# Weight-block sums moved from VectorE and ScalarE to GpSimd in a hybrid decoder step

## The chip, the cores and the metric

The kernel runs on one core of a Trainium2 chip. A core has five engines with an instruction queue each: TensorE (PE in the profile) multiplies matrices from SBUF into PSUM, VectorE (DVE) and ScalarE (ACT) work on tiles element by element, GpSimd (POOL) also works on tiles and issues DMA transfers, SyncE (SP) issues DMA transfers. The engines run side by side and wait for each other through semaphores; each takes its own queue in order.

The metric is the device time of one execution in microseconds, as the median of several runs. The profile is that of one execution.

## The reference

One inference step of one decoder layer, for a prompt of 2048 rows and for 8 sample rows with given states; the model width is 1024:

```python
hn = _rmsnorm(x, g_norm) * (1.0 + scale[:, None]) + shift[:, None]
z = hn @ w_in                      # columns: xa, za (RG-LRU), q, k, v, glr, zg (gated linear attention)
...
y_lru = h.astype(x.dtype) * jax.nn.silu(za)
...
y_gla = o.reshape(Bn, T, D_GLA).astype(x.dtype) * jax.nn.silu(zg)
mix = jnp.concatenate([y_lru, y_gla], axis=-1) @ w_out
x = x + gate[:, None] * mix
```

All is float32 with a close tolerance. `w_in` is 1024 x 5136, `w_out` is 2048 x 1024. Between the two products stand a short convolution, two gates and a recurrence (group one), and a chunked causal attention with decay (group two).

## The kernel before

**Precision.** A float32 product is made of three fast products: each operand is split into a high part (a cast to a rounded type, `F32R`) and a low part (the operand less its high part), and high x high, high x low and low x high are added up in PSUM. So a "split" of a tile is a cast and a subtraction.

**Fewer products.** Some matrix products are done on 2 x 2 blocks with seven block products in place of eight. That needs sums and differences of weight blocks, split like everything else. They are prepared on the side, early in the program, and written to DRAM, from where later stages load them:

- `pair_weights` (line 764) prepares five pairs of input-weight column tiles. For each pair it loads the four blocks b11, b21, b12, b22 (each 128 x 512) into the tile `tr`, forms four differences in place (line 776), and splits each of the four results: cast into `th` (line 781), subtraction in place (line 782), and two DMAs to the DRAM tile `twd` (line 784). The blocks are read again from about 610 us on.
- `out_weights` (line 800) prepares the output weights in 16 steps s = 0 to 15. A step loads two row tiles of `w_out` into `r` (line 829), multiplies them by the gate `g` (two operations on 512 columns, line 850), forms four differences on 256 columns (line 850, into `t` and `r`), and writes seven blocks to the DRAM tile `wd` (line 864). Every step with s // 4 odd (eight of them) also splits two blocks: casts into `p` (line 854), subtractions (line 855), DMAs to `wd2` (line 857). Before steps 0, 7 and 8 the gate is loaded again and its bias added (line 815).

**The order of the work.** The program is written out by Python and the order on each engine follows mostly from the order of writing, with a planner that may move what is ready. Side work is put in by a clock of the writing, not of the chip: every projection (24 products of 128 x 512 or less) advances it by one unit or half a unit (`tick`), and `after(units, f)` calls `f` at the first tick at or past the time asked for. `pair_weights` and `out_weights` are chains of such calls: load, four units later the first group of operations, then the next. Step s + 1 loads when step s has issued its stores; the tiles `r` and `t` have one buffer.

Two helpers tie side work to a place in another engine's queue. Both take the last instruction written so far for that engine as the mark:

```python
def behind(q):
    return tc.issue_after(next(x for x in reversed(list(nc.cur_bb.bb.instructions)) if x.engine == q.engine))
...
def held(q):
    mark = next(x for x in reversed(list(traced)) if x.engine == q.engine)
    ...
    for x in list(traced):
        if id(x) not in before and x.engine in (SP.engine, G.engine):
            tc.add_manual_dep(x, mark.name, ...DependencyClass.Sync...)
```

`behind(V)` keeps a VectorE instruction from being planned ahead of the VectorE instruction written before it; it adds no wait. `held(V)` makes each SyncE and GpSimd instruction of its block wait by semaphore for that VectorE instruction.

**The stages in time.** First half of the rows: four heads of attention, each followed by some tiles of the recurrence. The pairs are prepared from 77 us on (loads at 77.3 to 279.9 us), the steps follow from 310.9 us. Before the second half the memory is laid out anew (`open_sp`, line 1460): the tiles of steps and pairs end, and the first block of the second half, `fs`, lies where `r` and `p` were. `next_hn` (line 1428) fills it through `modulate` (lines 197 to 205): transposes on PE, scaling on ACT (lines 199 and 201) or DVE (203), a cast on GpSimd (204), the low part on DVE (205). Then come the seven-product stages of the second half (line 1567, products at 1561), which read `twd`; then the second half's attention heads with the remaining steps; then the output product (line 1846), which reads `wd` and `wd2`.

**What else the lines in this text are.** Lines 147 to 153 are a reciprocal square root in some eleven tiny DVE operations, 181 scales rows by it, 228 and 225 are the low part and the cast of the first half. The attention's chain is 999 (running sum of the decay), 1027 (scaled queries), 1042 (products of queries and keys), 1049 (low part of the masked scores), 1072 to 1077 (output and state products and the state's update), 1081 (output copied from PSUM), 1089 (its norm), 1162 (its transposes). The samples' chain runs over 1098 and 1100 (loads issued by GpSimd), 1105, 1114, 1124 to the product in line 1164. The gate columns come back through line 1210, a GpSimd DMA. Line 1303 is the low part of the convolution's output.

Of the kernel before, what the change touches and what calls it, by code (L numbers as in the profile page):

```python
# [8 lines left out]
F32 = mybir.dt.float32  # L9
# [3 lines left out]
OP = mybir.AluOpType  # L13
# [36 lines left out]
def dram(ap, off, pattern):  # L50
    return bass.AP(tensor=ap.tensor, offset=ap.offset + off, ap=pattern)
# [3 lines left out]
def hybrid_kernel(ctx, tc, i, o):  # L55
    nc = tc.nc
    V, S, G, PE, SP = nc.vector, nc.scalar, nc.gpsimd, nc.tensor, nc.sync
# [623 lines left out]
    def behind(q):  # L681

        return tc.issue_after(next(x for x in reversed(list(nc.cur_bb.bb.instructions)) if x.engine == q.engine))


    @contextmanager
    def held(q):

        traced = nc.cur_bb.bb.instructions
        mark = next(x for x in reversed(list(traced)) if x.engine == q.engine)  # L690
        before = {id(x) for x in traced}
        yield
        for x in list(traced):
            if id(x) not in before and x.engine in (SP.engine, G.engine):
                tc.add_manual_dep(x, mark.name, mybir.DependencyInfo(
                    mybir.DependencyClass.Sync, mybir.DependencyReason.DATA), reason="held")
# [4 lines left out]
    def after(units, fn, gla=False, val=False):  # L701
        clock[1] += 1
        heapq.heappush(pend, (clock[0] + units, clock[1], fn, gla, val))
# [46 lines left out]
    def ready(what):  # L750
        nonlocal hp
        waiting.remove(what)
        if what == "pairs":
            hpx.close()
            hp = hpx.enter_context(tc.tile_pool(name="hp", bufs=1, reuse_waits="tile"))
        if not waiting:
            out_weights()

    def zpairs():

        return ([(ZG + 2 * h * P, ZG + (2 * h + 1) * P) for h in HEADS[1:]]
                + [(ZA + j * P, XA + j * P) for j in EARLY])

    def pair_weights(n=0):

        cols = zpairs()
        if n == len(cols):
            ready("pairs")
            return
        r = hp.tile([P, 2, KT, P], F32, tag="tr", name="tr")  # L770
        for a, col in enumerate(cols[n]):
            G.dma_start(r[:, a], i["w_in"][0, :, col:col + P].rearrange("(k p) n -> p k n", p=P))
        b11, b21, b12, b22 = r[:, 0, :4], r[:, 0, 4:], r[:, 1, :4], r[:, 1, 4:]

        def sub(x, y, z):
            return lambda: V.tensor_tensor(x, y, z, op=OP.subtract)

        def split(k, x):
            def f():
                t = hp.tile([P, 4, P], F32R, tag="th", name="th", bufs=2)  # L780
                S.copy(t, x)
                V.tensor_tensor(x, x, t.bitcast(F32), op=OP.subtract)
                for u, y in enumerate((t.bitcast(F32), x)):
                    G.dma_start(twd[n, k, :, u], y.rearrange("p k n -> p (k n)"))
            return f

        def one(ops):
            for f in ops[0]:
                with behind(V):
                    f()  # L790
            if ops[1:]:
                after(0.5, lambda: one(ops[1:]))
            else:
                pair_weights(n + 1)

        halves = [split(k, x) for k, x in enumerate((b11, b22, b12, b21))]
        after(4, lambda: one([[sub(b11, b12, b11), sub(b12, b22, b12), sub(b22, b22, b11), sub(b21, b21, b22)],
                                halves[:2], halves[2:]]))

    def out_weights(s0=0):  # L800


        def begin(s):
            q = s // 8
            outw["busy"] = True

            g = hp.tile([P, 2, 256], F32, tag="g", name="g")
            bt = hp.tile([P, 2, 256], F32, tag="t", name="bt")
            G.dma_start(g, dram(gated, (8 + 32 * q) * 256, [[0, P], [64 * 256, 2], [1, 256]]))
            G.dma_start(bt, dram(i["b_ada"], 2 * D + q * 256, [[0, P], [512, 2], [1, 256]]))  # L810
            r = load(s)

            def add():
                with behind(V):
                    V.tensor_tensor(g, g, bt, op=OP.add)
                after(0.5, lambda: step(s, r, g))

            after(4, add)

        def where(s):  # L820

            return s // 8, s // 4 % 2, s % 4

        def load(s):
            q, f, m = where(s)
            r = hp.tile([P, 2, 2, 256], F32, tag="r", name="r")
            for a in range(2):
                k = CTS[f] + 4 * a + m
                G.dma_start(r[:, a], i["w_out"][0, k * P:(k + 1) * P].rearrange("p (b n) -> p b n", b=2)[:, :, q * 256:q * 256 + 256])
            return r  # L830

        def one(ops, end):


            with behind(V):
                for f in ops[0]:
                    f()
            if ops[1:]:
                after(0.5, lambda: one(ops[1:], end))
            else:  # L840
                end()

        def step(s, r, g):
            t = hp.tile([P, 3, 256], F32, tag="t", name="t")
            b11, b12, b21, b22 = r[:, 0, 0], r[:, 0, 1], r[:, 1, 0], r[:, 1, 1]
            q, f, m = where(s)
            c = slice(q * 256, q * 256 + 256)

            def op(*a):
                return lambda: V.tensor_tensor(*a[:3], op=a[3])  # L850

            def split(n, x):
                p = hp.tile([P, 2, 256], F32R, tag="p", name="p", bufs=2)
                S.copy(p[:, 0], x)
                V.tensor_tensor(p[:, 1], x, p[:, 0].bitcast(F32), op=OP.subtract)
                for h in range(2):
                    G.dma_start(wd2[n, :, h, m, c], p[:, h].bitcast(F32))

            def store():

                for x, ops in ((r[:, 0], (B11, T1)), (r[:, 1], (B21, B22)), (t, (T2, T3, T4))):
                    for n, k in enumerate(ops):
                        if not (f and k in (B22, T4)):
                            G.dma_start(wd[f, k, :, m, c], x[:, n])
                if outw["stop"] or s == 15:
                    outw["busy"], outw["next"] = False, s + 1
                elif s % 8 < 7:
                    again(s + 1, g)
                elif q == 0:
                    begin(s + 1)  # L870

            one([[op(r[:, 0], r[:, 0], g, OP.mult), op(r[:, 1], r[:, 1], g, OP.mult)],
                 [op(t[:, 1], b22, b12, OP.subtract), op(b12, b12, b11, OP.subtract),
                  op(t[:, 0], b22, b12, OP.subtract), op(t[:, 2], b21, t[:, 0], OP.subtract)]]
                + ([[lambda: split(0, b22), lambda: split(1, t[:, 2])]] if f else []), store)

        def again(s, g):
            r = load(s)
            after(4, lambda: step(s, r, g))

        begin(s0)
# [846 lines left out]
    class Pair:  # L1728
# [157 lines left out]
        def end(self, t):  # L1886
            V.scalar_tensor_tensor(self.z[t], self.z[t], self.r[:, t:t + 1], gfin, op0=OP.mult, op1=OP.mult)
# [288 lines left out]
    for n in range(2, 16):  # L2176
        g = n - 1
        x, prev = pairs[n], pairs[n - 1]
# [16 lines left out]
    for q in range(8):  # L2195
        g, k = 2 + q // 2, q % 2
# [63 lines left out]
```

## Time and profile before

| | us |
|---|---|
| median of 3 runs | 1455.29 (1455.26 to 1460.6) |
| the profiled execution's own time | 1454.69 |
| its span, first to last instruction | 1452.9 |

| engine | busy us | share of the span |
|---|---|---|
| PE | 1424.1 | 98% |
| PE weight load | 1250.8 | 86% |
| DVE | 1051.5 | 72% |
| ACT | 689.6 | 47% |
| POOL | 220.0 | 15% |

The granted clock of TensorE is 0.998 over the run. Busy time of POOL counts both its arithmetic and the making of its DMA issues (about 0.54 us each for the stores of lines 784, 857 and 864). A row of a group gives its line, engine, operation, the tiles written and read, the shape and the count; a row of a line's own view gives the durations as min/median/max in ns and the first and last start in us. A row of waits names who waited, for whom, and then the total in us, the count and the longest. A wait is put down to the instruction that ended it last.

### The profile page before, as it was taken

How to read it: one execution, taken by the hardware profiler on the slowest of the kernel's cores; microseconds unless marked ns; L12 is line 12 of the kernel's file. 1: busy time of each engine (PE TensorE's matmuls, PEld its weight loads, DVE VectorE, ACT ScalarE, POOL GpSimd, SP SyncE). 2: the span in 40 equal slices, each digit the busy share in tenths (PEclk: the TensorE clock that was granted, in tenths of full speed). 3: DMA queues.
4: the chain of work that ended last, by engine and by line, in shares of the span. 5: the costliest groups of instructions: out<-in, count | busy, mean ns of one | idle time of the engine just before them, and what ended most of it. 6: DMA issues, size and time to landing. Idle time of an engine off the chain costs nothing. (4 is left out here: it accounts for less than half of the span.)

```text
span 1452.9 us, 23584 instructions
## 1 busy us (share of the span) xinstructions
PE 1424.1 (98%) x8741; PEld 1250.8 (86%) x8741; DVE 1051.5 (72%) x2477; ACT 689.6 (47%) x1251; POOL 220.0 (15%) x364
## 2 busy tenths in 40 slices
PE   7999999999999999999999999999999999999998
PEld 5888989899898988778999999999998887788886
DVE  5757657776676688955468687586788986688886
ACT  4644544662545358524353454535557622144342
POOL 0200111212122113100212322323100000000000
PEclk9999999999999999999999999999999999999999
DMA  9755775764666455667846565656562767694453
GB/s 328 268 185 175 260 262 203 249 236 165 199 209 203 148 179 207 207 221 237 292 158 201 186 217 184 220 186 209 184 226 83 276 221 272 232 362 131 139 171 116
DMA packets 161752, 305.33 MB, mean 210 GB/s; under 512 B 12962, under 2 KB 91458, under 8 KB 159197
## 3 DMA queue, kind: packets, MB, share of 16 engines
q1 hardware_dynamic: 106837, 217.39, 43.6%
q0 software_dynamic: 22752, 70.44, 14.3%
q10 hardware_dynamic: 32048, 16.00, 3.7%
q8 instruction: 69, 1.13, 0.3%
q14 instruction: 46, 0.38, 0.1%
HBM read 188.51 MB, written 115.33 MB: 209 GB/s over the span
## 5 line engine op out<-in xcount | busy, mean ns | idle before, releaser
L661 PE MATMUL acc<-hh,w 128*128 128x512 f32 (+3 forms) x1112 | 386.1, 347 | 0.5 <-DVE xb L999 0.2
L662 PE MATMUL acc<-hl,w 128*128 128x512 f32 (+3 forms) x1112 | 375.6, 338 | 0.2 <-DVE hl L205 0.2
L663 PE MATMUL acc<-hh,w 128*128 128x512 f32 (+3 forms) x1112 | 375.1, 337 | 0.0
L662 PEld LDWEIGHTS acc<-hl,w 128*128 128x128 f32 x1112 | 209.3, 188 | 18.1 <-issue 1.2
L661 PEld LDWEIGHTS acc<-hh,w 128*128 128x128 f32 x1112 | 209.2, 188 | 18.1 <-ACT tx L1318 0.9
L663 PEld LDWEIGHTS acc<-hh,w 128*128 128x128 f32 x1112 | 209.1, 188 | 16.3
L1846 PE MATMUL acc<-w,a 128*128 128x512 f32 (+1 forms) x792 | 184.8, 386 | 0.0
L1846 PEld LDWEIGHTS acc<-w,a 128*128 128x128 f32 x792 | 146.8, 188 | 33.2 <-issue 3.4
L346 PE MATMUL acc<-w,hh 128*128 128x256 f32 (+1 forms) x508 | 144.7, 285 | 0.0
L348 PE MATMUL acc<-w,hl 128*128 128x256 f32 (+1 forms) x508 | 143.5, 282 | 0.2 <-DVE hl L228 0.2
L347 PE MATMUL acc<-w,hh 128*128 128x256 f32 (+1 forms) x508 | 143.4, 282 | 0.0
L1846 PE MATMUL tp<-w,a 128*128 128x512 f32 x564 | 136.0, 391 | 0.0
L1846 PEld LDWEIGHTS tp<-w,a 128*128 128x128 f32 x564 | 105.2, 188 | 26.8 <-issue 5.2
L346 PEld LDWEIGHTS acc<-w,hh 128*128 128x128 f32 x508 | 95.5, 188 | 1.3 <-ACT zs L1128 0.4
L348 PEld LDWEIGHTS acc<-w,hl 128*128 128x128 f32 x508 | 96.2, 189 | 0.4 <-DVE hl L228 0.4
L347 PEld LDWEIGHTS acc<-w,hh 128*128 128x128 f32 x508 | 96.0, 189 | 0.2
L1128 ACT ACTIVATE zs<-acc 128x512 f32<-128x512 f32 (+3 forms) x70 | 34.3, 490 | 107.0 <-PE acc L663 104.0
L1696 ACT CAST a<-s 128x512 fp32r<-128x512 f32 x61 | 36.5, 619 | 96.1 <-issue 36.6
L1278 DVE SCALAR_TENSOR_TENSOR cv<-xa,vecT,cv 128x512 f32<-128x512 f32 (+2 forms) x120 | 76.3, 638 | 7.2 <-ACT cv L1276 6.7
L1129 DVE SCALAR_TENSOR_TENSOR zs<-zs,acc 128x512 f32<-128x512 f32 (+3 forms) x70 | 38.4, 548 | 46.7 <-ACT zs L1128 46.7
L957 ACT CAST vh<-acc 128x256 fp32r<-128x256 f32 x56 | 20.5, 369 | 94.2 <-PE acc L348 81.8
L958 DVE TENSOR_TENSOR vl<-acc,vh 128x256 fp32r<-128x256 f32 x56 | 23.3, 420 | 51.1 <-ACT vh L957 51.1
(403 smaller groups left out, 2746.4 us busy)
## 6 DMA issues: line engine op xcount, KB each, us to landing
parts<-w SPq DMA_DIRECT2D x37, 1024.0 KB
w<-parts SPq DMA_DIRECT2D x28, 1024.0 KB
wr<-in_w_in_dram SPq DMA_DIRECT2D x38, 512.0 KB
a<-mixd SPq DMA_DIRECT2D x63, 256.0 KB
w<-wd SPq DMA_DIRECT2D x12, 1024.0 KB
w<-twd SPq DMA_DIRECT2D x20, 512.0 KB
mixd<-zs ACTq DMA_DIRECT2D x34, 256.0 KB
wada<-in_w_ada_dram SPq DMA_DIRECT2D x16, 512.0 KB
```

The source lines that it names most:

```text
L346: PE.matmul(ps, hh[:, kt, c], hi[:, kt % 4], start=kt == 0, stop=False)
L347: PE.matmul(ps, hh[:, kt, c], lo[:, kt % 4], start=False, stop=False)
L348: PE.matmul(ps, hl[:, kt, c], hi[:, kt % 4], start=False, stop=kt == KT - 1)
L661: PE.matmul(ps[:, :n], hi[:, kt], a, start=kt == 0, stop=False)
L662: PE.matmul(ps[:, :n], hi[:, kt], b, start=False, stop=False)
L663: PE.matmul(ps[:, :n], lo[:, kt], a, start=False, stop=kt == KT - 1)
L958: V.tensor_tensor(lo, ps[:, :DV], hi.bitcast(F32), op=OP.subtract)
L1128: S.activation(z, ps, AF.Tanh, scale=0.5)
L1129: V.scalar_tensor_tensor(z, z, 1.0, ps, op0=OP.add, op1=OP.mult)
L1278: V.scalar_tensor_tensor(cv[:, cq], xa[:, cq.start + k:cq.stop + k], cw[k], cv[:, cq], op0=OP.mult, op1=OP.add)
L1696: S.copy(t[:, 0, k], (low(t) if src is None else src)[:, k])
L1846: PE.matmul(ps, t[:, u, k], w[:, v, k, c], start=(q < 3 or ps is own) and (k, u, v) == (0, 0, 0), stop=(k, u) == (3, 1), skip_group_check= ...
```

## The change

The four differences and the four splits of a pair, and all arithmetic of an output-weight step, are issued to GpSimd. A cast, which was a copy by ScalarE, becomes a GpSimd `tensor_scalar` that multiplies by 1.0 and adds 0.0. The blocks are written under `held(V)` instead of `behind(V)`: each GpSimd instruction in them, the DMA issues included, waits for the VectorE instruction written last before the block. In the pairs a whole group stands in one such block, and the groups follow each other after one unit of the clock instead of half a unit. Tiles, shapes, loads and stores stay as they are.

```diff
--- before.py
+++ after.py
@@ -773,23 +773,23 @@
         b11, b21, b12, b22 = r[:, 0, :4], r[:, 0, 4:], r[:, 1, :4], r[:, 1, 4:]
 
         def sub(x, y, z):
-            return lambda: V.tensor_tensor(x, y, z, op=OP.subtract)
+            return lambda: G.tensor_tensor(x, y, z, op=OP.subtract)
 
         def split(k, x):
             def f():
                 t = hp.tile([P, 4, P], F32R, tag="th", name="th", bufs=2)
-                S.copy(t, x)
-                V.tensor_tensor(x, x, t.bitcast(F32), op=OP.subtract)
+                G.tensor_scalar(t, x, 1.0, 0.0, op0=OP.mult, op1=OP.add)
+                G.tensor_tensor(x, x, t.bitcast(F32), op=OP.subtract)
                 for u, y in enumerate((t.bitcast(F32), x)):
                     G.dma_start(twd[n, k, :, u], y.rearrange("p k n -> p (k n)"))
             return f
 
         def one(ops):
-            for f in ops[0]:
-                with behind(V):
+            with held(V):
+                for f in ops[0]:
                     f()
             if ops[1:]:
-                after(0.5, lambda: one(ops[1:]))
+                after(1, lambda: one(ops[1:]))
             else:
                 pair_weights(n + 1)
 
@@ -811,8 +811,8 @@
             r = load(s)
 
             def add():
-                with behind(V):
-                    V.tensor_tensor(g, g, bt, op=OP.add)
+                with held(V):
+                    G.tensor_tensor(g, g, bt, op=OP.add)
                 after(0.5, lambda: step(s, r, g))
 
             after(4, add)
@@ -832,7 +832,7 @@
         def one(ops, end):
 
 
-            with behind(V):
+            with held(V):
                 for f in ops[0]:
                     f()
             if ops[1:]:
@@ -847,12 +847,12 @@
             c = slice(q * 256, q * 256 + 256)
 
             def op(*a):
-                return lambda: V.tensor_tensor(*a[:3], op=a[3])
+                return lambda: G.tensor_tensor(*a[:3], op=a[3])
 
             def split(n, x):
                 p = hp.tile([P, 2, 256], F32R, tag="p", name="p", bufs=2)
-                S.copy(p[:, 0], x)
-                V.tensor_tensor(p[:, 1], x, p[:, 0].bitcast(F32), op=OP.subtract)
+                G.tensor_scalar(p[:, 0], x, 1.0, 0.0, op0=OP.mult, op1=OP.add)
+                G.tensor_tensor(p[:, 1], x, p[:, 0].bitcast(F32), op=OP.subtract)
                 for h in range(2):
                     G.dma_start(wd2[n, :, h, m, c], p[:, h].bitcast(F32))
```

## The prediction

> **What bounds the kernel now.** I read the page first (part 1), then the busy time of each engine by stage, then the list of who made TensorE wait, then the rows of the lines that move.
>
> ```profile
> PE 1424.1 (98%) x8741; PEld 1250.8 (86%) x8741; DVE 1051.5 (72%) x2477; ACT 689.6 (47%) x1251; POOL 220.0 (15%) x364
> ```
>
> The columns below are stretch, its length, then busy time and count of PE, PEld, DVE, ACT and POOL, the granted clock, DMA share and GB/s.
>
> ```profile
> 143.00:304.00 161.00, 159.74 (x1067) 143.39 (x1066) 114.42 (x238) 82.62 (x143) 31.20 (x53) 1.00 0.73 241
> ...
> 318.00:549.00 231.00, 231.00 (x1287) 201.72 (x1286) 158.96 (x351) 111.10 (x185) 42.20 (x74) 1.00 0.56 185
> 549.00:600.00 51.00, 49.23 (x292) 42.55 (x291) 44.15 (x89) 38.99 (x66) 12.89 (x16) 1.00 0.52 189
> ...
> 760.00:1026.00 266.00, 261.58 (x2021) 251.37 (x2021) 201.97 (x656) 127.37 (x267) 85.42 (x146) 1.00 0.63 205
> 1026.00:1100.00 74.00, 71.58 (x478) 67.78 (x477) 60.04 (x193) 43.39 (x92) 4.99 (x8) 1.00 0.51 174
> ```
>
> TensorE is the bound nearly everywhere: 98% of the span. The work that moves lies in three stages: the input pairs (143 to 304), the first seven steps of the output weights (318 to 549) and the other nine (about 760 to 1026). In these PE is idle 1.3, 0.0 and 4.4 us. So the whole prize in them is under 6 us. Who caused it, first in 143 to 304, then in 713 to 1030 (total, times, longest); in 318 to 549 the list is empty:
>
> ```profile
> PE tp L1042 <- DVE xb L1027: 1.0, 1, 1.0
> PE tp L1162 <- DVE on L1089: 0.3, 1, 0.3
> ...
> PE tp L1164 <- DVE os L1124: 1.6, 3, 0.5
> PE po L1072 <- DVE on L1081: 1.5, 2, 1.0
> PE tp L1042 <- DVE xb L1027: 0.6, 1, 0.6
> PE acc L661 <- DVE xb L999: 0.2, 1, 0.2
> PE po L1074 <- DVE aml L1049: 0.2, 1, 0.2
> ```
>
> All of it is DVE, 1.3 and 4.1 us: short chains of the attention group, late behind something else on DVE. None is ACT or POOL. So the question is what the change does to DVE.
>
> **What it removes.** The rows give count, then min/median/max in ns.
>
> ```profile
> L776 DVE TENSOR_TENSOR tr<-tr x20: 679/685/693, 143.6 to 291.6; 128x512 f32<-128x512 f32 x20
> L782 DVE TENSOR_TENSOR tr<-tr,th x20: 680/684/686, 147.7 to 303.0; 128x512 f32<-128x512 f32 x20
> L815 DVE TENSOR_TENSOR g<-g,bt x3: 681/682/683, 319.6 to 800.0; 128x512 f32<-128x512 f32 x3
> L850 DVE TENSOR_TENSOR r<-r,g x32: 668/684/693, 328.0 to 1014.2; 128x512 f32<-128x512 f32 x32
> L850 DVE TENSOR_TENSOR t<-r x32: 410/417/426, 329.8 to 1023.2; 128x256 f32<-128x256 f32 x32
> L850 DVE TENSOR_TENSOR r<-r x16: 410/418/426, 330.5 to 1022.4; 128x256 f32<-128x256 f32 x16
> L850 DVE TENSOR_TENSOR t<-r,t x16: 414/417/426, 332.7 to 1023.9; 128x256 f32<-128x256 f32 x16
> L855 DVE TENSOR_TENSOR p<-r,p x8: 415/418/419, 464.2 to 1023.5; 128x256 fp32r<-128x256 f32 x8
> ...
> L781 ACT CAST th<-tr x20: 599/621/625, 144.3 to 297.0; 128x512 fp32r<-128x512 f32 x20
> L854 ACT CAST p<-r x8: 395/406/409, 460.2 to 1014.9; 128x256 fp32r<-128x256 f32 x8
> ```
>
> From DVE go 40 x 0.685 = 27.4 us of the pairs, and of the steps 3 x 0.682 + 32 x 0.684 + 64 x 0.417 + 16 x 0.418 = 2.0 + 21.9 + 26.7 + 6.7 = 57.3 us (a step splits two blocks, so line 855 has as many rows for t as for r): 84.7 us. From ACT go 20 x 0.621 + 16 x 0.406 = 18.9 us, and the time ACT stands in front of these casts, since ACT runs in order. No PE wait in these stages is put down to ACT, so I take this gain as nothing: what hides it is PE itself, which has its operands.
>
> **What it adds to POOL.** The trace has one-input POOL arithmetic only, here in 560 to 596 us:
>
> ```profile
> L204 POOL TENSOR_SCALAR hh<-fs x12: 618/806/1454, 562.8 to 594.1; 128x512 fp32r<-128x512 f32 x12
> L204 POOL TENSOR_SCALAR hh<-ra x4: 617/619/622, 577.6 to 589.8; 128x512 fp32r<-128x512 f32 x4
> ```
>
> An undisturbed cast of 512 columns is 0.62 us; I take 0.31 for 256. A two-input operation does not occur. Lower bound: as one input, 0.62. Upper bound: two reads, each as slow as the slowest row, 2 x 1.454 = 2.9. I take two undisturbed reads, 1.24 us (0.62 for 256 columns), nearest to the four rows that nothing disturbed. Pairs: 40 x 1.24 + 20 x 0.62 = 62 us. Steps: 35 x 1.24 + 80 x 0.62 + 16 x 0.31 = 98 us. Sum 160 us, between 89 (all as one-input casts) and 375. POOL would be busy 93 of 161 us among the pairs and 85 + 55 = 140 of 266 in the last stage, so at 160 us it keeps up.
> [...]
>
> **What that does to DVE.** The same stretch shows DVE operations that grow while POOL works. Last columns: busy us, mean ns; idle before.
>
> ```profile
> L205 DVE TENSOR_TENSOR hl<-fs,hh 128x512 fp32r<-128x512 f32 x12 | 9.0, 753 | 1.3 <-POOL hh L204 1.3
> L181 DVE TENSOR_SCALAR xst<-xst,rs 128x1024 f32<-128x1024 f32 x5 | 4.6, 963 | 0.0
> L151 DVE TENSOR_TENSOR rs_t<-rs_y 128x2 f32<-128x2 f32 x9 | 2.8, 307 | 0.2
> L152 DVE SCALAR_TENSOR_TENSOR rs_t<-rs_t,rs_x 128x2 f32<-128x2 f32 x9 | 1.9, 206 | 0.3
> L153 DVE SCALAR_TENSOR_TENSOR rs_y<-rs_t,rs_y 128x2 f32<-128x2 f32 x6 | 1.4, 226 | 0.1
> ...
> L181 DVE TENSOR_SCALAR xt<-xt,rs 128x1024 f32<-128x1024 f32 x1 | 0.7, 734 | 0.0
> L153 DVE SCALAR_TENSOR_TENSOR rs<-rs_t,rs_y 128x2 f32<-128x2 f32 x3 | 0.5, 161 | 0.1
> ```
>
> Against 0.684 for the 512-column subtraction, 0.734 for the scaling and 0.161 for the tiny operations, DVE lost 12 x 0.069 + 5 x 0.229 + 9 x 0.146 + 9 x 0.045 + 6 x 0.065 = 0.8 + 1.1 + 1.3 + 0.4 + 0.4 = 4.0 us while POOL had 16 x 0.62 = 9.9 us of work of its own: 0.41 us per us. On 160 us that is 66 us back, so DVE ends 19 us lighter, 2 of them in the pairs and 17 in the steps: about 1 to 3 points of its share. The ends are 0 (85 us lighter) and 1 (75 us heavier); I take 0.41 because it is the only row. What a point of DVE share is worth shows across the stages above: DVE at 69% of a stage goes with no PE idle time, 71% with 0.8%, 76% with 1.7%, 81% with 3.3%, 87% with 3.5%. A few points off 266 us are worth about 1 us: term **-1 us**.
>
> **Order and waits.** The casts and differences of a pair used to come in three groups half a unit of the program's clock apart, now one unit apart. Where the calls advance the clock by a whole unit this is the same thing, since a group fires at the next call. Followed through the calls, only the last pair comes one unit later, all seven steps after it too, and the nine later steps not at all. A unit there:
>
> ```profile
> L829 POOL DMA_DIRECT2D r<-in_w_out_dram x4: 704/721/731, 310.9 to 335.2; - x4
> ...
> L829 POOL DMA_DIRECT2D r<-in_w_out_dram x2: 717/722/728, 514.8 to 515.5; - x2
> ```
>
> Step 0 loads at 310.9, step 6 at 514.8, 33 units: 6.2 us each. Steps 0 to 5 are wanted hundreds of us later. Step 6 must be gone before line 199 writes the first block of the second half into the same memory:
>
> ```profile
> L857 POOL DMA_DIRECT2D wd<-p x4: 540/541/557, 543.7 to 547.7; - x4
> DMA to landing us min/median/max: 2.0/6.0/6.7
> L199 ACT ACTIVATE fs<-tp,Sh,Gm x12: 563/566/604, 561.7 to 590.4; 128x256 f32<-128x256 f32 x12
> ```
>
> The last store lands at 547.7 + 6.7 = 554.4, 7.3 us before 561.7. The delay is between 3 us (POOL's step of 2 x 1.24 + 4 x 0.62 + 2 x 0.31 + 2 x 0.62 = 6.8 us for DVE's 3.9) and 9.2 us (a unit more). So 0 to 2 us of PE time; I take 0, because both the step before and the step after hang on the same DVE instruction, not on the unit.
> The held POOL instructions wait for the VectorE instruction traced before them, where DVE's own stood before; behind them on POOL's queue are the step's stores, the loads of the sample states and of the gate columns. Before, those stood behind the same DVE results, so the added delay is a step's 3 us. Only the sample chain meets PE without slack (line 1164, 0.5 us each); one of its chains lies beside a step. Term **+1 us**, bounds 0 and 3. No DMA is added, none changes queue, and SP gets no wait.
>
> **Sum.** 1454.7 (this execution's own time; span 1452.9 plus 1.8 around it) - 1 + 1 = 1454.7, and the median of the runs, 1455.3, is 0.6 above it: **1455.3 us**, no change. Half a per cent, 7.3 us, is what I count as a difference.
>
> **Rivals.** *The shared way into SBUF decides (slower).* If DVE stands still for all of POOL's 160 us, it gets 62 - 27 = 35 us heavier among the pairs (149 of 161, 93%), 43 - 25 = 18 in the first seven steps (177 of 231, 77%), 55 - 32 = 23 in the last nine (225 of 266, 85%). By the shares above PE's idle time becomes 3.5% of 161, 1.7% of 231 and 3.4% of 266: 5.6 + 3.9 + 9.0, less the 5.7 it has, so +13 us: **1468 us**. It sets in where DVE loses more than 84.7 / 160 = 0.53 us per us of POOL. For it speaks that two-input operations hold longer and come four in a row; against it that many DVE rows here read PSUM and that 0.41 was measured where DVE was 87% busy.
> [...]
> *DVE's relief reaches PE (faster).* If all PE waits on DVE in these stages go, 1.3 + 4.1 = 5.4 us: **1449.9 us**; short of half a per cent unless waits too short for the list go with them. Against it: the waits follow PE's own results through single PSUM buffers, not the moved work.
> *The hand-over at 561.7 fails*: POOL at its upper price (375 us, 2.3 times) would make step 6 16 us long, PE late by up to 16 - 3.9 + 6.2 - 7.3 = 11 us: **1466 us**. This is the same unknown, POOL's price, so I count it with the first.
>
> **Chances.** Forecast 0.62; the slower rival with the hand-over 0.20, of which 0.17 beyond half a per cent; the faster one 0.18, of which 0.06 beyond. So faster 0.06, same 0.77, slower 0.17. The range for 8 in 10 leaves out the last tenth on each side: 1449 to 1467 us; the likeliest case's own is 1452 to 1460.
>
> **What would show it.** Right: PE's idle time in the three stages stays under 8 us together; DVE near 1030 us, ACT near 670, POOL near 380; two-input rows of POOL near 1.24 us. Wrong: rows of lines 151, 181 and 1303 grown among the pairs, PE waiting for DVE in 318 to 549, line 199 waiting for the stores of line 857, or a reordered VectorE queue, which the planner of the instruction order may give and nothing here can show.

## The result and the profile after

The changed kernel takes **1478.4 us** (median; 1477.8 to 1479.6), beside 1457.9 us for the kernel before on the same chip: ratio 1.0132, 95% interval 1.0089 to 1.0175. So the change costs some 20 us, where none had been forecast. The profiled execution took 1479.55 us, its span is 1477.7, that is 24.8 us more than the span before (one execution of each; by the medians it is the 20 us above).

The busy time of the engines, from the page of the changed kernel:

```profile
PE 1432.3 (97%) x8741; PEld 1253.8 (85%) x8741; DVE 1052.2 (71%) x2322; ACT 672.4 (46%) x1215; POOL 411.0 (28%) x555
```

155 instructions worth 84.7 us left VectorE, and its busy time is what it was: 1052.2 against 1051.5. So 85.4 us came back as longer VectorE instructions, beside 411.0 - 220.0 = 191 us of new GpSimd work: 0.45 us for each. TensorE's own idle time went from 1452.9 - 1424.1 = 28.8 to 1477.7 - 1432.3 = 45.4 us, and its busy time rose by 8.2 us: 16.6 + 8.2 = 24.8.

The same by stage (columns as in the prediction: stretch, its length, busy time and count of PE, PEld, DVE, ACT and POOL, granted clock, DMA share, GB/s); the last two rows are two short stretches inside the first:

```profile
143.00:310.00 167.00, 157.96 (x1009) 139.71 (x1008) 108.13 (x193) 70.89 (x121) 85.33 (x91) 0.97 0.66 218
330.00:560.00 230.00, 226.65 (x1263) 197.52 (x1263) 156.31 (x308) 105.02 (x175) 89.86 (x123) 1.00 0.59 194
...
777.00:1050.00 273.00, 263.34 (x2027) 251.42 (x2026) 204.06 (x593) 124.57 (x260) 146.04 (x212) 1.00 0.60 199
242.40:245.80 3.40, 3.40 (x18) 3.40 (x17) 3.18 (x6) 0.98 (x3) 3.33 (x5) 0.50 0.91 330
286.80:293.60 6.80, 5.33 (x12) 3.86 (x13) 6.76 (x7) 1.93 (x3) 6.65 (x9) 0.50 0.46 173
```

Two things are to be seen. TensorE is now idle for 9.0, 3.4 and 9.7 us in the three stages (before 1.3, 0.0 and 4.4), while VectorE is no busier in any of them than before: 65%, 68% and 75% of the stage, against 71%, 69% and 76%. And among the pairs the granted clock was 0.50 for 3.4 and for 6.8 us, where the kernel before had 1.00 for that whole stage. In those 10.2 us TensorE was busy for 8.7 us, 3.4 and 5.3. Products of 256 columns started every 0.21 us in the first (0.12 at a clock of 1.00), products of 512 columns every 0.43 us in the second (0.23), so by estimate the two cost 3.4 x (1 - 0.12 / 0.21) + 5.3 x (1 - 0.23 / 0.43) = 3.9 us: nearly half of the 8.2 us by which TensorE's busy time rose.

Setting the start of the k-th matrix product of one trace against that of the other shows where the delay comes in: none until 224 us of the changed kernel, which is even 1.7 us ahead there, 12.9 us by 304, 15.3 by 356, no more until 520, 18.0 by 626, and the rest, 6.8 us, in pieces of 1 to 2.6 us to 1062. So half of it falls into 80 us. Who made TensorE wait there, from the lists of waits in 225 to 260, 260 to 300 and 300 to 350 (total, times, longest):

```profile
PE po L1072 <- DVE on L1081: 3.5, 1, 3.5
PE tp L1162 <- DVE on L1089: 1.7, 1, 1.7
...
PE acc L1315 <- ACT xh L1302: 2.8, 1, 2.8
PE acc L1316 <- DVE xl L1303: 1.1, 1, 1.1
...
PE tp L1042 <- DVE xb L1027: 2.4, 1, 2.4
```

Behind the third and fourth row stands this stretch of the timeline (start, duration, engine, line, operation, tiles; in brackets the idle time before it and what ended it):

```profile
271.35 9.82 POOL L776 TENSOR_TENSOR tr<-tr 128x512 f32<-128x512 f32 x4 [4.46 <-DMA tr<-in_w_in_dram]
272.25 2.31 DVE L305 TENSOR_TENSOR w<-wr,w 128x1024 fp32r<-128x1024 f32 x1
...
276.84 3.27 DVE L1334 TENSOR_TENSOR_SCAN tg<-xl,tx 128x1024 f32<-128x1024 f32 x1
280.02 1.18 DVE L1341 TENSOR_TENSOR tg<-xl,vecT 128x8 f32<-128x8 f32 x1
...
282.64 2.55 ACTq L675 DMA_DIRECT2D mixd<-zs  x3
285.23 0.58 ACT L1394 COPY xa<-acc 128x512 f32<-128x512 f32 x1 [10.40 <-DMA mixd<-zs]
286.39 1.96 DVE L679 COPY mixs<-zs 128x8 f32<-128x8 f32 x1
```

GpSimd and VectorE are both slower here: four subtractions of 1.29 us each by their median (below) take 9.82 us, and on VectorE a subtraction of 1.22 us takes 2.31, and two operations on 8 columns, of 0.16 and 0.17 us by their medians, 1.18 and 1.96. ScalarE stands 10.4 us before it takes the next product out of PSUM: ahead of that on its queue are three stores of `zs` (line 675), which VectorE writes only at the end of its lengthened row of operations (line 1352, 281.9 to 284.8). TensorE runs out of work. Rows of single lines, count with min/median/max in ns; the last one is of the kernel before:

```profile
L776 POOL TENSOR_TENSOR tr<-tr x20: 1281/1294/3144, 143.8 to 321.2; 128x512 f32<-128x512 f32 x20
...
L850 POOL TENSOR_TENSOR r<-r,g x32: 1268/1307/2341, 349.2 to 1043.0; 128x512 f32<-128x512 f32 x32
L850 POOL TENSOR_TENSOR t<-r x32: 732/748/1114, 354.4 to 1048.9; 128x256 f32<-128x256 f32 x32
...
L999 DVE TENSOR_TENSOR_SCAN xb<-xb x64: 392/399/3198, 63.4 to 1055.1; 128x128 f32<-128x128 f32 x64
...
L999 DVE TENSOR_TENSOR_SCAN xb<-xb x64: 391/400/760, 63.4 to 1030.0; 128x128 f32<-128x128 f32 x64
```

Behind the first wait, of 3.5 us up to 241.3, stands a queue:

```profile
232.41 5.37 POOL L776 TENSOR_TENSOR tr<-tr 128x512 f32<-128x512 f32 x4 [5.24 <-DMA tr<-in_w_in_dram]
237.72 0.58 POOL L1153 DMA_DIRECT2D zgd<-zq  x1
239.51 0.18 ACT L1128 ACTIVATE zq<-acc 128x8 f32<-128x8 f32 x1 [7.32 <-DMA zgd<-zq]
239.72 0.16 DVE L1129 SCALAR_TENSOR_TENSOR zq<-zq,acc 128x8 f32<-128x8 f32 x1 [7.26 <-ACT zq L1128]
```

A small store of the sample's gate (line 1153) is issued by GpSimd. It now stands behind four subtractions, which themselves stand 5.2 us for their load. Its tile has one buffer, so ScalarE waits 7.3 us to write the next one, VectorE waits 7.3 us for ScalarE, and TensorE's 3.5 us follow.

### The profile page after: what moved, and what is told of

It reads as the page before. It is cut to its first block, busy times and chain, and to the rows that moved or that the text cites. A ratio compares the mean times of both kernels' runs of the same rounds, so it can differ in the third digit from the quotient of the medians.

```text
span 1477.7 us, 23458 instructions
## 1 busy us (share of the span) xinstructions
PE 1432.3 (97%) x8741; PEld 1253.8 (85%) x8741; DVE 1052.2 (71%) x2322; ACT 672.4 (46%) x1215; POOL 411.0 (28%) x555
## 5 line engine op out<-in xcount | busy, mean ns | idle before, releaser
L1278 DVE SCALAR_TENSOR_TENSOR cv<-xa,vecT,cv 128x512 f32<-128x512 f32 (+2 forms) x120 | 83.4, 697 | 7.3 <-ACT cv L1276 6.8
L850 POOL TENSOR_TENSOR r<-r,g 128x512 f32<-128x512 f32 x32 | 46.9, 1488 | 89.8 <-DVE xl L1303 21.7
```

Of the source, the lines that this page charges most:

```text
L850: return lambda: G.tensor_tensor(*a[:3], op=a[3])
L1278: V.scalar_tensor_tensor(cv[:, cq], xa[:, cq.start + k:cq.stop + k], cw[k], cv[:, cq], op0=OP.mult, op1=OP.add)
```

## The experiments

Three theories. **P**: GpSimd's reads of SBUF hold VectorE's instructions, and it costs time where such a hold falls on a short chain between two products of TensorE. **Q**: the cost lies in GpSimd's queue, in what stands behind the long operations (the store of line 1153 first of all). **O**: the cost lies in how the moved work is now ordered, spaced and waited for, whichever engine does it.

### Each half alone

e1_pairs_only has the changed pair sums and the steps of before; e2_steps_only the reverse.

```
e1:  pair_weights as after, out_weights as before
e2:  pair_weights as before, out_weights as after
```

> Pairs as in the changed kernel, steps as before. Theory P (the shared way into SBUF holds DVE operations while GpSimd works) and theory Q (a small GpSimd store of the gate's sample columns, line 1153, stands behind GpSimd arithmetic, and ScalarE waits for its landing) both put most of the loss among the pairs: the delay of the PE instructions against before grows by about 15 of the 25 us there, so 1470 us (1468 to 1473). Theory O (the planner's order or the new grouping, not the engine) expects no such split and rather the whole loss or none, 1455 or 1478.

> Steps as in the changed kernel, pairs as before. P: the other 9 to 10 us, 1464 us (1461 to 1467), with the running sums of line 999 and the small operations grown beside the steps. Q: nothing, since the line 1153 stores beside the steps were not waited for, 1455 to 1457. O: 1455 or 1478.

Measured: pairs alone 1471.3 us, ratio 1.0103 (1.0081 to 1.0125); steps alone 1464.6, ratio 1.0055 (1.0037 to 1.0073). The two add up to 1.0158, inside the interval of the whole change. Both halves cost; the pairs cost two thirds of it with 290.2 - 220.0 = 70 us of GpSimd's time, the steps one third with 341.1 - 220.0 = 121. So the price does not go by the amount. Nor can the store of line 1153 be all of it: in the steps alone, 8 of the 10.7 us of delay come in after 784 us, and the last of those stores is issued at 510.

### The store of line 1153

```
-  q = xp.tile([P, NS], F32, tag="rs_y", name="zq", bufs=1)
+  q = xp.tile([P, NS], F32, tag="rs_x" if ct % 2 else "rs_y", name="zq", bufs=1)
```

The changed kernel with two buffers for that tile in turn; every engine has its instructions in the same order as without the edit.

> The changed kernel, but the two gate columns of a head use two tiles that exist already, in turn, so the second does not wait for the first one's store. Q: the delay between 224 and 262 us goes, 7.7 us of which 1.7 are the lower granted clock, so 1470 to 1474 us and no wait of line 1128 for zgd. P: that place is DVE held up by the four differences anyway, 1476 to 1479 us.

Measured: 1476.9 us, ratio 1.0134 (1.0108 to 1.0159): in the time it can't be told from the changed kernel. In the profile the mechanism is there: the wait of 3.5 us is gone, the delay at 280 us is 2.1 us where it was 6.0, the first stretch at half clock is gone too, and the span is 1474.8 against 1477.7. So Q is real; at this store it is worth about 3 us of the 24.8 between the two profiles, which the medians (1476.9 and 1478.4) neither show nor rule out.

### GpSimd busy, but without reading

In e5_no_reads each two-input operation of the changed kernel becomes two fills of its output and each cast one (the sums are left out); in e7_three_fills three fills, which together take longer than the operation they stand for (1.6 us for 1.29). In short form:

```
-  G.tensor_tensor(x, y, z, op=OP.subtract)
+  for k in range(2): G.memset(x, float(k))      # e7: range(3)
```

> The changed kernel, but each GpSimd operation on two inputs becomes two fills of its output tile and each cast one fill, so the weight sums are left out and GpSimd reads no SBUF; the queue, the waits and the stores stay, a 512-column pair of fills takes about 1.04 us (a fill of that size took 0.52) in place of 1.29. P: the losses at 271 to 300 us, 330 to 345 us and beside the steps go, the one at 224 to 262 us stays: 1460 to 1465 us, and rows of lines 305 and 999 back at 1.22 and 0.42 us. Q alone or O: still 1470 us or more.

> As the run with two fills, now three for each two-input operation: about 1.6 us in place of 1.29 for 512 columns and 0.93 in place of 0.75 for 256, so GpSimd's queue is blocked longer than in the changed kernel, without its reads; the sums are left out. P (reads): still near the run with two fills, 1450 to 1457 us. If GpSimd's occupied time and queue are the cause: above the changed kernel, 1478 us or more; halfway if both.

Measured: e5 1452.3 us, ratio 0.9971 (0.9959 to 0.9983), faster than before; e7 1459.9, ratio 1.0015 (1.0005 to 1.0025). Neither is where P had put it: e5 is below its 1460 to 1465, since the wait behind the store of line 1153, which was to stay, is gone too, and e7 is 3 us above its 1450 to 1457. First the page of e5, then that of e7, then e7's row of the table by stage:

```profile
PE 1425.4 (98%) x8741; PEld 1251.1 (86%) x8741; DVE 1003.3 (69%) x2322; ACT 673.0 (46%) x1215; POOL 346.9 (24%) x710
```

```profile
PE 1425.4 (98%) x8741; PEld 1251.8 (86%) x8741; DVE 1008.8 (69%) x2322; ACT 672.5 (46%) x1215; POOL 402.3 (28%) x865
```

```profile
143.00:304.00 161.00, 160.99 (x1081) 145.18 (x1080) 97.20 (x199) 71.64 (x123) 84.42 (x165) 1.00 0.71 234
```

In e7 GpSimd is as busy as in the changed kernel (402.3 against 411.0), the order on VectorE, ScalarE and SyncE is that of the changed kernel, and the spacing of the pairs and the waits for held instructions are the same. Of the 1.3% a tenth is left. Among the pairs GpSimd is busy for 84 us, as in the changed kernel, and TensorE is busy for all but 0.01 of 161 us, at full clock; between 140 and 340 us the list of its waits is empty, in e5 as in e7. VectorE ends 43 us lighter than in the changed kernel, yet 42 us heavier than the moved work alone would leave it (1051.5 - 84.7 = 966.8): fills hold VectorE as well, 0.23 us for each of theirs (0.29 in e5), but among the pairs not where TensorE waits. What differs is that GpSimd reads nothing (and that the second half multiplies by constants, which can't touch the stretch before 304 us). That speaks against O and against Q as the main cause. It does not clear Q altogether: the wait behind the store of line 1153 is 2.1 us here, where the changed kernel has 7.3, and e7, whose fills occupy GpSimd 55 us longer than those of e5, costs 0.4% more than e5. Here is the row of a VectorE line that kept its time in e7, and that of one that did not; the third is of the kernel before:

```profile
L999 DVE TENSOR_TENSOR_SCAN xb<-xb x64: 392/400/759, 63.2 to 1031.2; 128x128 f32<-128x128 f32 x64
...
L1078 DVE TENSOR_SCALAR S<-S,f x60: 341/348/2085, 97.1 to 1063.1; 128x256 f32<-128x256 f32 x60
...
L1078 DVE TENSOR_SCALAR S<-S,f x60: 341/346/411, 97.3 to 1061.9; 128x256 f32<-128x256 f32 x60
```

The scan with two inputs never took more than 0.76 us (3.20 in the changed kernel, 0.76 in the kernel before), while the scaling of one tile by a column did take up to 2.09 us (0.41 before). What sets the two apart was not shown; in e13 below line 1078 took at most 0.42 us.

### The same reads, for nobody

The test in the other direction: the kernel before keeps all its work, and GpSimd does the pairs' operations once more on a spare tile. In short form, with the mix of casts left out:

```
+  spare = hp.tile([P, 512], F32, tag="spare", bufs=1)
   for f in ops[0]:
       with behind(V): f()
+  with held(V):          # e10: 4 operations; e13: three memsets for each, one for a cast
+      G.tensor_tensor(spare, spare, spare, op=OP.mult)
```

> The kernel before, which keeps all its sums on VectorE and ScalarE, and beside each group of a pair the GpSimd operations that the change put there, on a spare tile that nobody waits for: 20 times four two-input operations or two casts and two two-input operations of 512 columns in all 40 x 1.29 + 20 x 0.63 = 64 us. VectorE, ScalarE and TensorE keep their order, nothing waits for GpSimd. Theory P (GpSimd's reads hold VectorE's short chains between TensorE's products, and nothing else is needed): as slow as the change of the pairs alone or slower, since VectorE also keeps 27 us that it lost there: 1466 to 1485 us, with the clock at half for some us between 230 and 310. Theory O (the cause is in the moved work: its order, its waits, its stores): 1455 to 1459 us.

> The same, with three fills of the spare tile (0.53 us each) for every two-input operation and one for a cast: some 40 x 1.6 + 20 x 0.5 = 74 us of GpSimd that reads nothing. Theory P: 1454 to 1460 us, against 1466 to 1485 for the reads. Theory O: the same as the reads, 1455 to 1459.

Measured: with reads 1474.0 us, ratio 1.0125 (1.0108 to 1.0142); with fills 1463.6, ratio 1.0051 (1.0035 to 1.0067). In both, TensorE, VectorE, ScalarE and SyncE have their instructions in the order of before, and nothing waits for the spare tile. GpSimd's busy time is 291.8 and 293.5 us. With reads it costs as much as the change of the pairs did (1.0103), with none of the work moved, so O is not needed. But not all of that is the reads: 0.5% remains when GpSimd is kept as busy without them. The reads' own part is the difference, 10.4 us. One place in the timeline of e10:

```profile
186.61 3.97 DVE L999 TENSOR_TENSOR_SCAN xb<-xb 128x128 f32<-128x128 f32 x4
187.00 4.42 POOL L646 TENSOR_TENSOR spare<-spare 128x512 f32<-128x512 f32 x4
...
191.67 0.21 ACT L1008 ACTIVATE f<-f 128x5 f32<-128x5 f32 x1 [4.22 <-DVE f L1005]
...
195.60 2.08 PE L1042 MATMUL tp<-xb,e 128*128 128x128 f32 x8 [5.06 <-DVE xb L1027]
```

The same place in the kernel before, and then in e13:

```profile
183.41 1.37 DVE L999 TENSOR_TENSOR_SCAN xb<-xb 128x128 f32<-128x128 f32 x4
...
189.14 1.16 PE L1042 MATMUL tp<-xb,e 128*128 128x128 f32 x8 [0.96 <-DVE xb L1027]
```

```profile
183.82 1.36 DVE L999 TENSOR_TENSOR_SCAN xb<-xb 128x128 f32<-128x128 f32 x4
184.02 4.03 POOL L646 MEMSET spare<- 128x512 f32 x7
...
189.74 1.16 PE L1042 MATMUL tp<-xb,e 128*128 128x128 f32 x8 [1.14 <-DVE xb L1027]
```

In e10 the four scans take 3.97 us beside four multiplications of GpSimd, for 1.37 before; the chain of lines 999, 1005, 1008, 1011, 1021, 1027 is late, and TensorE stands 5.1 us at its end, for 1.0. Beside seven fills, in e13, the scans take what they took before, and TensorE stands 1.1 us. That is P, at one place, with the same instructions on every other engine. Elsewhere e13 was not free:

```profile
309.12 10.49 POOL L646 MEMSET spare<- 128x512 f32 x18
...
321.21 1.42 POOL L829 DMA_DIRECT2D r<-in_w_out_dram  x2
...
326.93 0.69 DVE L815 TENSOR_TENSOR g<-g,bt 128x512 f32<-128x512 f32 x1 [3.50 <-DMA r<-in_w_out_dram]
...
328.28 2.08 PE L1042 MATMUL tp<-xb,e 128*128 128x128 f32 x8 [3.29 <-DVE xb L1027]
```

P had expected 1454 to 1460 us for e13, and e13 lost 4.9 us here at once. Eighteen fills had piled up on GpSimd's queue, and the loads of gate, bias and weights (lines 809, 810 and 829) stood behind them; the last was issued at 321.2 (before at 310.9, and e13 ran only 4 us late there). VectorE, whose instructions stay in order, stood 3.5 us for them with the chain of line 1027 behind, and behind TensorE's wait of 3.3 us eight products of line 1042 took 2.08 us, for 1.16 before: by estimate at a clock near half, since 1.16 / 2.08 = 0.56 is about the 0.12 / 0.21 = 0.57 of the stretch at 0.50 above. That is Q's mechanism at another place.

### Shorter operations

Each two-input operation of the changed kernel in pieces of 128 columns, so that no single operation of GpSimd is long. In short form:

```
-  G.tensor_tensor(x, y, z, op=op)
+  for u, v, w in pieces(x, y, z, 128): G.tensor_tensor(u, v, w, op=op)
```

> The changed kernel with each two-input GpSimd operation cut into pieces of 128 columns (four or two for one); same elements read, more instructions. P with a hold for each instruction: a waiting VectorE operation gets in after 0.3 to 0.4 us and not after 1.3, so DVE loses less per instruction and time falls to 1462 to 1472 us, or, if the next piece takes the way in again before DVE does, it stays at 1476 to 1490 us. If only the sum of GpSimd's reading time counted: 1478 us or a little more.

Measured: 1482.4 us, ratio 1.0158 (1.0131 to 1.0184), no better than the change and perhaps worse. A piece takes 0.46 us by the median, four of them 1.83 us for 1.29. The page, and the row of the pairs' first operation:

```profile
PE 1435.5 (97%) x8741; PEld 1256.9 (85%) x8741; DVE 1033.8 (70%) x2322; ACT 673.2 (45%) x1215; POOL 473.4 (32%) x851
```

```profile
L646 POOL TENSOR_TENSOR tr<-tr x80: 443/458/2448, 143.4 to 332.5; 128x128 f32<-128x128 f32 x80
```

VectorE did end 18 us lighter than in the changed kernel, and TensorE did not gain by it: again a VectorE total that says nothing of the time.

### The spacing of the pairs

The change also lets the groups of a pair come one unit apart in place of half a unit. Two kernels have that spacing with VectorE and ScalarE doing the work. e4_pacing takes the change's helper as it is, which drops `behind(V)`; e9_one_unit keeps it and alters the number alone.

```
e4:  -  for f in ops[0]:            e9:  -  after(0.5, lambda: one(ops[1:]))
     -      with behind(V): f()          +  after(1, lambda: one(ops[1:]))
     +  with held(V):
     +      for f in ops[0]: f()
     +  after(1, lambda: one(ops[1:]))
```

> Engines as before the change (VectorE and ScalarE), but the pairs with the changed kernel's order helper, one group of operations at a time and one unit between groups. P (GpSimd's reads hold VectorE): as before, 1453 to 1459 us. O (the new grouping and pacing cost it): 1465 us or more.

> The kernel before with the groups of a pair one unit of the program's clock apart in place of half a unit; VectorE and ScalarE do the sums and keep their places by behind. Theory P: no difference, 1454 to 1459 us. Theory O (the later last pair and the later seven steps cost time by themselves): 1460 to 1468 us.

Measured: e4 1495.9 us, ratio 1.0264 (1.0248 to 1.0279); e9 1468.3, ratio 1.0091 (1.0076 to 1.0106). P missed both, and O's numbers came true (1465 or more, and, to 0.3 us, 1460 to 1468); but e4 costs twice as much as the whole change, and the causes are in VectorE's waits. e4, in 80 to 340:

```profile
DVE tr L776 <- DMA tr<-in_w_in_dram: 33.4, 3, 13.8
```

and e9 in the timeline, first the second load of a pair, then the subtraction that needs it:

```profile
177.31 0.90 POOL L772 DMA_DIRECT2D tr<-in_w_in_dram  x1 [4.29 <-issue]
...
184.53 0.69 DVE L776 TENSOR_TENSOR tr<-tr 128x512 f32<-128x512 f32 x1 [6.84 <-DMA tr<-in_w_in_dram]
```

In e4 the planner, no longer held to the program's place, put the sums far ahead in VectorE's queue (the first starts at 95 us, before at 144), and VectorE stood 33 us for their loads. In e9 the second pair's loads go out 10 us later than before (167.24), and VectorE stands 14.5 us for them in all (0.7 before). So the late spacing is dear where VectorE stands in the wait. In the changed kernel it is GpSimd that stands there (the 5.24 and 4.46 us before line 776 in the two stretches of its timeline above), and e7, with that spacing and GpSimd in that wait, costs 0.15%. So O's numbers are right where VectorE does the sums, and O does not explain the change.

### Casts alone, and another moment

e6_casts_only moves only the casts to GpSimd; e12_unit_later is the changed kernel with a pair's sums five units after its loads in place of four.

```
e6:   -  S.copy(t, x)
      +  G.tensor_scalar(t, x, 1.0, 0.0, op0=OP.mult, op1=OP.add)
e12:  -  after(4, lambda: one(...))
      +  after(5, lambda: one(...))
```

> Before the change, with only the casts moved from ScalarE to GpSimd (20 of 512 and 16 of 256 columns, one input, 0.62 and 0.40 us). P by the sum of reading time: 19 us of 196 us of GpSimd arithmetic, a tenth of the loss, 2 to 3 us, set against ScalarE no longer standing in front of casts: 1454 to 1459 us. If the casts on GpSimd were the larger part of the loss: 1465 us or more.

> The changed kernel with each pair's sums five units after its load in place of four: as much work on GpSimd (411 us) and VectorE (1052 us) to 10 us, at other moments. If the amount of held work sets the price (the prediction's step, with another rate): 1475 to 1481 us. Theory P (the price depends on which chain a hold falls on): another time by 3 us or more, up or down, 1463 to 1474 or 1482 to 1492 us, with the delay of TensorE between 220 and 300 changed.

Measured: e6 1456.3 us, ratio 0.9995 (0.9984 to 1.0006): 17 us off ScalarE buy nothing, and 24 us more on GpSimd cost nothing. e12 1482.6 us, ratio 1.0187 (1.0172 to 1.0202), by its median 4.2 us above the changed kernel, with as much work:

```profile
PE 1433.9 (97%) x8741; PEld 1255.3 (85%) x8741; DVE 1048.4 (71%) x2322; ACT 672.5 (45%) x1215; POOL 410.2 (28%) x555
```

```profile
PE tp L1162 <- DVE on L1089: 6.6, 3, 5.4
```

Its delay comes in elsewhere: none at 290 us, where the changed kernel lost 6.9, but 8.9 us in one piece between 240 and 264 (the second fence is from its list of waits in 140 to 340), and 14.5 us after 626 us for the 6.8. The amount is the same and the places and the sum are not; that the difference in time, 4 us between kernels that were timed beside different runs of the one before, is of the size that P asked for, is weak support. The sign could not have been told beforehand.

No version that does the whole computation beats both kernels; e6 equals the one before.

## Why the prediction was wrong

**The bound.** Right: TensorE's 98%, and that the time hangs on short VectorE chains. The waits that grew among the pairs are on lines 1072, 1162, 1042, 1315 and 1316, four of the five for VectorE; the last two belong to a chain (lines 1278, 1302, 1303) that the list of before did not show at all, since nothing waited for it then.

**What leaves, and what GpSimd takes.** Right in kind, 31 us short. By the medians a two-input operation of 512 columns takes 1.29 us and one of 256 columns 0.75 us, for the 1.24 and 0.62 assumed; casts 0.63 and 0.41 for 0.62 and 0.31. With the holds the sum is 191 us for 160.

**What VectorE loses.** Right: 0.41 us for each of GpSimd's was forecast, 0.45 measured, and VectorE's total ended level where 19 us less had been forecast. That last is the product of two small misses and of no weight. That the rate came so near is in part luck: it was taken from a row of casts, and where casts alone were moved (e6) VectorE's total rose by 5.0 us for 24.3 us of GpSimd, 0.21 for each. What is left for the two-input operations is (85.4 - 5.0) / (191 - 24.3), so 0.48 by estimate.

**What that is worth in TensorE's time.** This is the step that failed. The prediction read across the stages that "VectorE at 69% of a stage goes with no PE idle time, 71% with 0.8%", and concluded that a few points are worth about 1 us. After the change the stages stand at 65%, 68% and 75% and have 5.4%, 1.5% and 3.5% of idle time, where it was 0.8%, none and 1.7%: fewer points, and more loss in each. The share counts VectorE's work as if it could be done at any time. What counts is whether one chain is late, and the change put delays of 1 to 3 us, several in a row, onto chains with little or no slack (line 999 took up to 3.20 us for 0.76, line 305 up to 4.23 for 1.29). At the place shown in e10, four scans that took 2.6 us longer stand ahead of a wait of TensorE that grew from 1.0 to 5.1 us. e10 beside e13 shows it without any of the moved work, e7 by taking the reads away, and e8 by making VectorE 18 us lighter to no use.

**The clock.** The prediction had no term for it. TensorE stood still from 237.8 to 241.3, and the granted clock was 0.50 from 242.4, when TensorE had been at work again for 1.1 us; it stood from 284.4 to 287.2, and the clock was 0.50 from 286.8, that is 2.4 us into a wait that ended 0.4 us later, with full work before it. The two stretches at half clock lasted 3.4 and 6.8 us and cost 3.9 us by the estimate above. Two other waits in this trace, 2.4 us up to 336.5 and 2.5 up to 1045.7, brought no half clock (1.00 from 336.5 to 345 and from 1045.7 to 1052). What makes the clock fall was not shown.

**Order and waits.** The term was +1 us with bounds of 0 and 3, and it named the step's stores and the loads behind GpSimd's work. The store of line 1153 was not among them; it is worth about 3 us by e3's profile, at the bound. The reading that of the pairs "only the last pair comes one unit later" was wrong as well: in e9, which alters that number alone, the second pair's loads start at 172.1 us for 160.9, and e9 costs 0.9%, some 13 us. In the changed kernel, where GpSimd stands in that wait, e7 shows that it does not cost this. The hand-over to line 199 was right: in the profile after, that line waits for TensorE alone.

**The rivals.** The one that came true in kind, VectorE held by GpSimd, stood at 0.20 and 1468 us, but on the condition that VectorE lose more than 0.53 us per us; at 0.45 it came true all the same, since the condition was drawn from the same mean. That the way into SBUF is what the two share was not shown; the runs show that GpSimd's reads of a tile cost 10.4 us more than fills (e10 less e13). The relief of VectorE was priced at 5.4 us, and e5, where VectorE ends 48 us lighter, got 1456.1 - 1452.3 = 3.8: the size was near, but it came with fills in place of the work.

**The signs named.** Of the three stages' idle time "under 8 us together" became 22.1. VectorE's total, near 1030, ScalarE's 670 and GpSimd's 380 came out as 1052, 672 and 411. Of the signs against, line 1303 grown among the pairs (at most 1.54 us for 0.69) and TensorE waiting for VectorE in 318 to 549 came (3.4 us, of which 2.4 stand at 336, where the last pair's operations now end); lines 151 (at most 0.18 us for 0.17) and 199 did not, and line 181 does not run among the pairs.

## What stays open

How the 24.8 us divide among P, Q and the clock is known only roughly. The store of line 1153 is about 3 us of it by e3's profile, the clock 3.9 us by estimate; the first of its two stretches is in both, since it is gone in e3. Q at other places has no number in the changed kernel; e13 (0.5% without reads) and e7 beside e5 (0.4%) say that it need not be small. For the reads among the pairs the nearest measure is e10 less e13, 10.4 us. For the steps only their sum (1.0055) was measured; that their pieces of about 1 us are all holds was read from rows such as the following, at 1041 us, not tested:

```profile
1041.33 3.83 DVE L999 TENSOR_TENSOR_SCAN xb<-xb 128x128 f32<-128x128 f32 x3
1041.71 2.52 POOL L850 TENSOR_TENSOR r<-r,g 128x512 f32<-128x512 f32 x2
...
1045.72 0.39 PE L1074 MATMUL po<-vh,aml 128*128 128x256 f32 x1 [2.52 <-DVE aml L1049]
```

## What to carry to other kernels

Work moved from VectorE to GpSimd was not gone from VectorE here: every us of it on GpSimd gave back 0.45 us, and fills, which read nothing, still gave back 0.23 to 0.29. Don't turn a share of busy time into time of the bounding engine; follow the shortest chain between two of its products, ask how many links of it can be held, and by how long an operation each. And look at every small DMA on the queue of the engine that gets the work, at how many buffers its tile has: behind the store of line 1153 ScalarE stood 7.3 us.

## What the runs showed of the hardware that was not expected

- Both engines lost time at once: four subtractions of 1.29 us took 9.82 us on GpSimd, while VectorE's operations on 8 columns took 1.18 and 1.96 us for 0.16 and 0.17.
- Beside GpSimd's fills in e7 the two-input scan of line 999 kept its time (at most 0.76 us, as before), while the scaling of line 1078 took up to 2.09 us for 0.41. In all, VectorE's time rose by 42 us for 182 us of fills in e7, and TensorE had no wait from it among the pairs.
- A two-input operation of GpSimd took 0.46 us at 128 columns, 0.75 at 256 and 1.29 at 512 by the medians, so by estimate about 0.2 us of it did not shrink with the size, and four pieces took 1.83 us for 1.29. (Six multiplications of one tile by itself in e10 took 1.12 us each on average, at 512.)
- The clock fell to half 2.4 us into one wait of TensorE, and stayed there for 6.8 us: more than twice the wait. A wait's length alone did not tell: one of 2.4 us up to 336.5 in the changed kernel brought no half clock, and around one of 2.4 us on line 1162 in e10 the mean clock of 225 to 260 us was 0.95.
